# The second pass of the scores of windowed attention on all 128 rows of the array, in a two-layer hybrid block

## The chip, the cores and the metric

The kernel runs on one core of a Trainium2 chip. The metric is the device time of one execution in microseconds. The engines are named as the profile names them: PE is TensorE (PEld its loads of stationary operands), DVE is VectorE, ACT is ScalarE, POOL is GpSimd, and SP issues the DMAs.

## What is computed

The reference is a block of two layers over 256 context tokens and 512 latent tokens of 1024 channels. In each layer the modulated rows go through an input projection into four groups of heads: windowed attention with sinks, retention, RWKV-7 and latent attention. Their outputs are joined and projected, and an MLP follows. The part that the change is about is the windowed attention, four query heads on two key heads of 64 channels:

```python
def sink_softmax(s, sink):
    m = jnp.maximum(jnp.max(s, axis=-1, keepdims=True), sink)
    p = jnp.exp(s - m)
    return p / (jnp.sum(p, axis=-1, keepdims=True) + jnp.exp(sink - m))
...
    s_loc = jnp.einsum('bnqhgd,bnkhd->bhgnqk', qb, kb).astype(jnp.float32)
...
    s_loc = jnp.where(valid, s_loc, -jnp.inf)
    s_ctx = jnp.einsum('bnqhgd,bchd->bhgnqc', qb, kc).astype(jnp.float32)
    probs = sink_softmax(jnp.concatenate([s_loc, s_ctx], axis=-1),
                         sink_hg[None, :, :, None, None, None]).astype(v.dtype)
```

Each block of 128 latent queries sees the keys of its own block, of the blocks beside it within a window of 128, and all 256 keys of the context. In the first layer the context's queries attend to the context as well.

## The kernel before

**Stages.** For each layer, `run` calls `mixers` (the input projection, beside the RWKV recurrence), `attention`, `out` (the output projection) and `mlp`. `attention` first merges three streams of instructions: the end of the recurrence (`Rwkv.tail`), `mla_prep` and `swa_prep`, which load, rotate and split the queries and keys of the two attentions. Then it merges three more, each in proportion to its share of the work: `mla` (latent attention), `swa` (windowed attention), and a chain of `Rwkv.finish`, `ret` (retention) and `w_out`. A scheduler orders each engine's instructions after that, and gives each tile a buffer of its pool when it is first written.

**Two passes in float32r.** A float32 operand is split into a high part, as float32r, and a low part, which is the rest. `swa_prep` builds for each of two blocks of query heads a tile `sq` of 128 rows with two blocks of columns: in block j, the high part of head j of the block on that head's 64 rows, and the low part on the other 64 rows (L883 and L884). For the keys it builds `skh`, in which block j holds the high part of key head j on both halves of the rows (L878, four casts of 64x768 on ACT), and `skl`, which holds the low part of both key heads, each on its own 64 rows (L879, two subtractions on DVE).

**Scores.** `swa` works by units: a block of query heads g, a tile of 128 tokens t, and a parity j. `scores` takes two banks of PSUM. Its inner function `products` issues two products for a range of keys: the first pass multiplies `sq` block j on all 128 rows with `skh` block j, so that high and low parts of the queries meet the keys' high part; the second pass multiplies the 64 rows of the queries' high part with the keys' low part. In both the queries are the stationary operand. A unit of context tokens (t below 2) has one such pair, over 256 columns; a unit of latents has two, over the 256 context columns and over the two or three blocks of latent keys (256 or 384 columns), and then one or two mask products of 128 columns in bfloat16, which add the window's bounds. There are 24 units in the first layer and 16 in the second. `softmax` follows: the row's maximum on DVE (L657), the exponential on ACT (L663, tile `prob`), and the normalisation on DVE. `attend` issues the scores of a unit ahead of the transposes of the one before (tile `pt`), and after each second unit the products with the values.

**Buffers and loads.** Tiles of 128 rows by two blocks of 768 columns come from one pool of 17 buffers (tag D), tiles of 1024 columns from another of 16 (tag B). In the attention the D tiles are those of both preparations, of `Rwkv.finish` (`fin`), of retention (`ret`), the outputs `y`, and at the end the gates and rows of the output stage. Loads stand in one queue, SP's, in a fixed order; a load waits until the last user of its buffer is done, and the loads behind it wait too. Retention's loads for a pair of heads are its values (L948), its keys (L949), its decays (L951), its queries twice (L954) and its gate (L955).

All matrix products go through the helper `mm` (L148), all transposes through `tp` (L151).

Of the kernel before, what the change touches and what calls it, by code (L numbers as in the profile page):

```python
# [8 lines left out]
F32 = mybir.dt.float32  # L9
# [3 lines left out]
ALU = mybir.AluOpType  # L13
# [12 lines left out]
# blocks of 128 columns of the input projection, as kernel() lays them out  # L26
# [4 lines left out]
# per-channel parameters, one row per block of 128 channels  # L31
# [4 lines left out]
# channels of a windowed head: the first of each rotary pair, then the second  # L36
# [3 lines left out]
def const_arrays():  # L40
    """Arrays that depend on shapes alone."""
# [51 lines left out]
    # retention, per pair of heads: decays inside a chunk, then those of the queries (forward on top of backward)  # L93
# [15 lines left out]
def merge(*streams):  # L109
    """emit generators side by side, each in proportion to its share of its total"""  # L110
    live = [[g, 0.0, float(tot)] for g, tot in streams]
    while live:
        z = min(live, key=lambda z: z[1] / z[2])
        try:
            z[1] += next(z[0])
        except StopIteration:
            live.remove(z)


def in_proportion(*streams):  # L120
    """like merge, as a generator"""
    live = [[g, 0.0, float(tot)] for g, tot in streams]
    while live:
        z = min(live, key=lambda z: z[1] / z[2])
        try:
            c = next(z[0])
            z[1] += c
            yield c
        except StopIteration:
            live.remove(z)  # L130
# [7 lines left out]
class Block:  # L138
# [15 lines left out]
    def rebank(self, one, two):  # L154
        """the first `one` banks serve requests for one bank, the pairs at `two` those for two"""
# [10 lines left out]
    def ptok(self):  # L166
        """two banks as 768 token columns: the context ends the first bank, the latents fill the second"""
        return self.pb()[:, 256:1024]

    def done(self, ps):  # L170
        """the instructions so far are the last on what pr, pb or ptok gave"""
# [6 lines left out]
    def D(self, name, dt=F32):  # L178
        """two blocks of 768 columns"""
# [15 lines left out]
    def split(self, hi, lo, src, lo_eng=None, pin=False):  # L195
        """src = hi + lo exactly, hi with float32r's significand; pin: not ahead of what the engine was given
        before, since src is still being loaded"""
# [9 lines left out]
    def rsqrt_small(self, ss, n, eps):  # L207
        """(ss / n + eps) ** -0.5 for a [128, k] tile"""
# [7 lines left out]
    def head_sums(self, squares, tiles, mul, add, add_op):  # L216
        """squares: [128, T] blocks (two heads each); (mul * sum over the head + add) ** -0.5 per token, head
        and block, as [128, block, head, tile]"""
# [12 lines left out]
    def head_rstd(self, sq, tiles, mul, add, add_op):  # L231
        """(mul * sum of the squares over the head + add) ** -0.5 on every channel of the head, in PSUM"""
# [5 lines left out]
    def on_channels(self, col, n, tiles):  # L238
        """columns of values per token as rows, each repeated over 128 / n channels, in PSUM"""
# [24 lines left out]
    def start(self):  # L264
        """constants, silu of the conditions, the normalised rows; then the loads of the first modulation, whose
        blocks of channels the projection takes as they come"""
# [12 lines left out]
        # silu(c) and silu(c_ctx), channel-major, padded to 32 columns  # L279
# [12 lines left out]
        # adds up the four groups of 32 rows, and picks the two conditions  # L292
# [27 lines left out]
        def modulation(k):  # L320
            """A and B of a block of channels: the rows of the weights in four groups side by side, then their sum"""
# [36 lines left out]
    def params(self, l):  # L358
        """per-channel parameters of layer l, one column per block of 128 channels"""
# [22 lines left out]
        # sinks of the four heads, on every partition  # L382
# [7 lines left out]
    def ada(self, parts, n):  # L390
        """modulation columns into DRAM, n of them from each (layer, first column): weights times silu on the
        vector engine and the sum over the partitions on the tensor engine"""
# [41 lines left out]
    def modulation(self, l, gname, src):  # L434
        """A = gain * (1 + scale), B = shift, channel-major, for latent and context"""
# [22 lines left out]
    def x_norm(self, x, xhat, sq):  # L458
        """xhat = x / rms(x) for a token tile"""
# [6 lines left out]
    def make_hT(self, hT, xh, mod, tl, room, blocks=range(8)):  # L466
        """channel-major hi | lo of the modulated rows of the token tiles tl; room: 1024 spare columns"""
# [17 lines left out]
    def load_w(self, src, shape, pool=None):  # L485
        """hi, lo tiles of a weight block"""
# [20 lines left out]
    def proj(self, ps, wh, wl, hT, segs):  # L507
        """ps[c, tok] = sum over channel blocks of W^T h, three passes; yields its share of the time"""
# [12 lines left out]
    def split_pair(self):  # L521
        """the first pair of banks serves requests for one bank from now on"""
# [21 lines left out]
    def in_spilled(self, l, hT, emit):  # L544
# [14 lines left out]
        def load(i):  # L559
            """the weights of block i of the order"""  # L560
# [5 lines left out]
        def prepare(i):  # L566
# [3 lines left out]
            if b == "kpe":      # the two halves side by side  # L570
# [9 lines left out]
        def ahead(b, g):  # L580
            """the products of block b, with the split of the next weights in their midst"""
# [42 lines left out]
        # rotary part of the keys  # L624
# [28 lines left out]
    def softmax(self, ps, n, nsink, sink, scale):  # L653
        """ps [128 q, n] scores -> normalised probabilities in SBUF"""
# [18 lines left out]
    def transposed(self, p, n):  # L673
        """[128, n] -> [128 keys, n/128, 128 q] in SBUF"""
# [14 lines left out]
    def token_major(self, dst, x, how="ident"):  # L689
        """[128 c, T] -> [128 tokens, 6, 128 c], as it is or without each head's mean"""  # L690
# [14 lines left out]
    def attend(self, units, scores, values):  # L705
        """units (key, parity): the scores of a unit are under way while the one before is transposed"""
# [16 lines left out]
    def mla_prep(self, l, emit):  # L723
# [16 lines left out]
        # the gain of q goes into the rows of w_uq, 1/rms (per token) into the softmax's scale  # L740
# [24 lines left out]
        def rotate(x, r):  # L765
            """the latents of x[r], in place"""
# [42 lines left out]
        # values, token-major  # L809
# [38 lines left out]
    def swa_prep(self, l, emit):  # L848
# [6 lines left out]
        def load(x, xp, src, t0):  # L855
            """as it is, and with the rotary pairs' members swapped"""
# [12 lines left out]
        kh, kl = self.D("skh", F32R), self.B("skl", F32R)[:, 0:T]  # L869
        qs = []  # L870
        for x, xp, t0 in ((k, xs[0], 0), (qq[:, 0], xs[1], tq0), (qq[:, 1], xs[2], tq0)):
# [3 lines left out]
            if t0 == 0 and x is k:  # L875
                for j, r in enumerate(half):
                    for r2 in (r, half[1 - j]):
                        nc.scalar.copy(kh[r2, j], k[r])  # L878
                    nc.vector.tensor_tensor(kl[r], k[r], kh[r, j].bitcast(F32), ALU.subtract)  # L879
            else:       # hi of a head where it is, lo on the other half of the partitions  # L880
# [9 lines left out]
    def swa(self, l, emit):  # L890
# [4 lines left out]
        def scores(key, j):  # L895
# [3 lines left out]
            r = slice(64 * j, 64 * j + 64)  # L899
# [3 lines left out]
            def products(out, keys, stop):  # L903
                self.mm(out, q, kh[:, j, keys], True, False)
                self.mm(out, q[r], kl[r, keys], False, stop)
# [27 lines left out]
    def ret(self, l, emit):  # L933
        """chunks of 128 tokens, both directions at once; the mean over a head's channels is taken from the
        values, which the outputs are linear in"""
# [886 lines left out]
```

## Time and profile before

| | |
|---|---|
| median of 3 runs | 2292.72 us (2283.75 to 2300.33) |
| span of the profiled execution, first to last instruction | 2293.7 us |
| PE busy | 2178.0 us, 95% of the span |
| DVE, ACT, POOL busy | 61%, 32%, 28% |
| attention, layer 0 and layer 1 | about 480 to 710 us and 1700 to 1885 us |

The profile tells the profiled execution's time as its span alone, which lies within the range of the three runs, 1.0 us above their median. Busy time counts an instruction from its start to its end. Products overlap in the array, so the time that one takes from the next is the step between their starts, which the timeline shows, and not its own duration. The granted clock of PE is given as a share: 1.0 is 2.4 GHz, 0.5 is 1.2 GHz.

### The profile page before, as it was taken

What the parts mean: (1) busy time and instruction counts of PE and PEld (TensorE: products, weight loads), DVE (VectorE), ACT (ScalarE), POOL (GpSimd) and SP (SyncE); (2) the same over time, 40 slices, a digit from 0 to 9 for tenths busy, and PEclk for the clock granted to TensorE, in tenths of its full rate; (3) what the DMA queues carried; (4) which work ended last, traced back from release to release, by engine and by line L of the source; (5) the groups of instructions that cost most, each with busy time, mean ns of one, the idle gap of its engine ahead of it and who ended that gap; (6) DMA issues with size and microseconds to landing.
All of it is one profiled execution on the core that took longest, in us unless ns stands there. A gap on an engine that the chain in (4) does not pass through costs nothing. (4 is left out here: it accounts for less than half of the span.)

```text
span 2293.7 us, 36538 instructions
## 1 busy us (share of the span) xinstructions
PE 2178.0 (95%) x14420; PEld 1671.5 (73%) x14420; DVE 1396.8 (61%) x2708; ACT 739.1 (32%) x1356; POOL 635.7 (28%) x711
## 2 busy tenths in 40 slices
PE   7998999989999999999999899999998999999997
PEld 4865666656667988888888686566666667888886
DVE  5488788767574766556555655777776555333334
ACT  3232222244443422222222333222233344332331
POOL 2443323240122311212112354322341013221321
PEclk9999999988899999999999999899999799999999
DMA  6322233431124444444343321111232123332232
GB/s 263 100 92 89 90 113 95 132 111 42 47 82 149 142 130 141 133 147 143 122 129 113 133 85 70 46 54 53 76 109 71 38 88 137 111 120 83 96 107 101
DMA packets 110889, 239.91 MB, mean 105 GB/s; under 512 B 22834, under 2 KB 49276, under 8 KB 110716
## 3 DMA queue, kind: packets, MB, share of 16 engines
q1 hardware_dynamic: 110716, 237.57, 31.6%
q8 instruction: 113, 1.85, 0.3%
q14 instruction: 60, 0.49, 0.1%
HBM read 206.93 MB, written 30.58 MB: 104 GB/s over the span
## 5 line engine op out<-in xcount | busy, mean ns | idle before, releaser
L148 PE MATMUL ps<-y,whi 128*128 128x512 f32 (+1 forms) x1664 | 422.1, 343 | 2.3 <-POOL y L482 1.0
L148 PE MATMUL ps<-whi,f 128*128 128x512 f32 x1280 | 401.0, 392 | 3.3 <-DVE f L1191 3.3
L148 PE MATMUL ps<-hT,whi 128*128 128x512 f32 (+3 forms) x1360 | 392.5, 370 | 5.2 <-ACT st L606 2.0
L198 ACT CAST whi<-wraw 128x1024 fp32r<-128x1024 f32 (+1 forms) x176 | 182.5, 1041 | 610.1 <-PE ps L148 377.7
L148 PEld LDWEIGHTS ps<-y,whi 128*128 128x128 f32 x1664 | 290.1, 190 | 42.6 <-POOL y L482 2.6
L148 PEld LDWEIGHTS ps<-hT,whi 128*128 128x128 f32 (+1 forms) x1360 | 232.9, 191 | 78.6 <-issue 37.8
L148 PE MATMUL ps<-y,wlo 128*128 128x512 f32 (+1 forms) x832 | 283.4, 342 | 0.7 <-POOL wlo L201 0.6
L148 PEld LDWEIGHTS ps<-whi,f 128*128 128x128 f32 x1280 | 240.9, 188 | 57.6 <-DVE f L1191 4.1
L201 POOL TENSOR_TENSOR wlo<-wraw,whi 128x1024 fp32r<-128x1024 f32 x57 | 141.1, 2475 | 428.8 <-ACT whi L198 403.2
L201 DVE TENSOR_TENSOR wlo<-wraw,whi 128x1024 fp32r<-128x1024 f32 x117 | 152.2, 1303 | 165.0 <-ACT whi L198 164.6
L148 PE MATMUL ps<-wlo,f 128*128 128x512 f32 x640 | 249.8, 390 | 0.0
L148 PE MATMUL ps<-hT,wlo 128*128 128x512 f32 (+1 forms) x648 | 233.7, 361 | 0.8 <-DVE wlo L201 0.8
L415 DVE SCALAR_TENSOR_TENSOR aacc<-aw,sil,aacc 128x768 f32<-128x768 f32 x140 | 162.2, 1204 | 27.6 <-ACT aacc L413 19.8
L148 PEld LDWEIGHTS ps<-y,wlo 128*128 128x128 f32 x832 | 157.8, 190 | 19.1 <-POOL wlo L201 0.8
L1190 POOL TENSOR_TENSOR fr<-fr 128x768 f32<-128x768 f32 (+1 forms) x64 | 92.9, 1451 | 272.0 <-ACT f L1189 265.4
L148 PEld LDWEIGHTS ps<-hT,wlo 128*128 128x128 f32 x648 | 125.3, 193 | 27.5 <-issue 11.7
L1191 DVE TENSOR_TENSOR f<-fr,f 128x768 fp32r<-128x768 f32 (+1 forms) x64 | 63.5, 992 | 123.7 <-POOL fr L1190 123.7
L148 PEld LDWEIGHTS ps<-wlo,f 128*128 128x128 f32 x640 | 120.6, 188 | 24.5
L1217 DVE TENSOR_TENSOR ya<-ya,ps 128x1024 f32<-128x1024 f32 x60 | 72.9, 1217 | 96.2 <-PE ps L148 96.2
L148 PE MATMUL ps<-wo,y 128*128 128x512 f32 x480 | 117.1, 397 | 3.8 <-POOL wo L201 1.9
L1604 DVE STREAM_TRANSPOSE Xp<-XY 32x128 f32<-32x128 f32 x384 | 115.8, 302 | 5.3
L148 PEld LDWEIGHTS ps<-wo,y 128*128 128x128 f32 x480 | 88.1, 188 | 25.3 <-ACT wo L198 4.0
(308 smaller groups left out, 3364.5 us busy)
## 6 DMA issues: line engine op xcount, KB each, us to landing
wraw<-in_w_b_dram SPq DMA_DIRECT2D x64, 512.0 KB
wraw<-in_mlp_w_dram SPq DMA_DIRECT2D x64, 512.0 KB
aw<-in_ada_w_dram SPq DMA_DIRECT2D x80, 384.0 KB
wraw<-in_w_in_b_dram SPq DMA_DIRECT2D x46, 512.0 KB
ada<-in_ada_w_dram SPq DMA_DIRECT2D x64, 192.0 KB
adaw<-in_ada_s_dram SPq DMA_DIRECT2D x16, 512.0 KB
wraw<-in_w_out_k_dram SPq DMA_DIRECT2D x32, 256.0 KB
xs<-x SPq DMA_DIRECT2D x16, 512.0 KB
```

The costliest lines, as they stand in the source:

```text
L148: self.nc.tensor.matmul(ps, lhsT, rhs, start=start, stop=stop)
L198: ins = self.nc.scalar.copy(hi, src)
L201: (lo_eng or self.nc.vector).tensor_tensor(lo, src, hi.bitcast(F32), ALU.subtract)
L415: nc.vector.scalar_tensor_tensor(a, w, sil, a, ALU.mult, ALU.add)
L1190: nc.gpsimd.tensor_tensor(fr, fr, fr, ALU.mult)
L1191: nc.vector.tensor_tensor(fl, fr, fh.bitcast(F32), ALU.subtract)
L1217: nc.vector.tensor_tensor(ya[t], ya[t], ps, ALU.add)
L1604: nc.vector.transpose(Xp[r, zz, b], Y[r, zz])
```

## The change

The keys' low part gets the layout of their high part: `skl` becomes a tile of the D pool with two blocks of columns, and block j holds the low part of key head j on both halves of the rows. DVE writes it on the head's own rows, as before, and ACT copies it to the other 64 rows. The second pass then multiplies all 128 rows of `sq` block j, the same stationary operand as the first pass has, with block j of `skl`. With it the product of both low parts, which was left out before, is added to the scores.

```diff
@@ swa_prep
-        kh, kl = self.D("skh", F32R), self.B("skl", F32R)[:, 0:T]
+        kh, kl = [self.D(nm, F32R) for nm in ("skh", "skl")]
@@
                 for j, r in enumerate(half):
                     for r2 in (r, half[1 - j]):
                         nc.scalar.copy(kh[r2, j], k[r])
-                    nc.vector.tensor_tensor(kl[r], k[r], kh[r, j].bitcast(F32), ALU.subtract)
+                    nc.vector.tensor_tensor(kl[r, j], k[r], kh[r, j].bitcast(F32), ALU.subtract)
+                    nc.scalar.copy(kl[half[1 - j], j], kl[r, j].bitcast(F32))
@@ swa, scores
-            r = slice(64 * j, 64 * j + 64)
             ps = self.ptok()
             q = qs[g][:, j, 128 * t:128 * t + 128]
...
             def products(out, keys, stop):
                 self.mm(out, q, kh[:, j, keys], True, False)
-                self.mm(out, q[r], kl[r, keys], False, stop)
+                self.mm(out, q, kl[:, j, keys], False, stop)
```

One line is added, so lines from L880 to the end of the scores stand one lower in the changed kernel until the removed line evens it out: the casts of the queries are L883 before and L884 after.

How instructions move: on PE, DVE and ACT the order changes only within the preparation of each layer; after it each engine has the same order as before. On ACT, in the preparation of the first layer, the rows before, from the casts of the keys on (`mla` belongs to latent attention, `ot` and P, T to the recurrence, `mqk` are the latent attention's queries):

```order
L878 CAST skh<-swa 64x768 x4
L762 COPY mla<-ps 128x768
L1695 COPY ot<-ps 128x256
L883 CAST sq<-swa 64x768 x2
L793 ACTIVATE mqk<-ps 64x768
L1671 COPY P_556<-ps 64x256
L793 ACTIVATE mqk<-ps 64x768
L1676 COPY T_558<-ps 64x256
L883 CAST sq<-swa 64x768 x2
L1695 COPY ot<-ps 128x256
```

and the same place in the changed kernel:

```order
L878 CAST skh<-swa 64x768 x4
L880 CAST skl<-skl 64x768
L762 COPY mla<-ps 128x768
L880 CAST skl<-skl 64x768
L1695 COPY ot<-ps 128x256
L884 CAST sq<-swa 64x768 x2
L793 ACTIVATE mqk<-ps 64x768 x2
L1671 COPY P_556<-ps 64x256
L884 CAST sq<-swa 64x768 x2
L1676 COPY T_558<-ps 64x256
```

The two added casts stand behind those of the keys, ahead of the first copy of `ot`, and the first two copies of `mqk` now stand together.

On SP, the loads of the recurrence's outputs and of the first pair of retention heads in the first layer, with what each waits for, before (DMAHW names other DMAs; a buffer's number stands in the tile's name):

```order
L1752 DMA fin_4895<-sp_rwv0_159 128x768 [waits DMAHW7_49,PE_49]
L1753 DMA fin_4895<-sp_rws0_160 128x768 [waits DMAHW0_49]
L948 DMA ret_5063<-sp_ret0_157 128x768 [waits DMAHW2_49,DMAHW1_49,DVE_49]
L949 DMA ret_5061<-sp_ret0_157 128x768 [waits PE_49]
L951 DMA ret_5061<-sp_ret0_157 128x768 [waits DMAHW3_49]
```

and in the changed kernel:

```order
L1752 DMA fin_4897<-sp_rwv0_159 128x768 [waits DMAHW4_49,DVE_49]
L1753 DMA fin_4897<-sp_rws0_160 128x768 [waits DMAHW0_49]
L948 DMA ret_5065<-sp_ret0_157 128x768 [waits DMAHW1_49,PE_49]
L949 DMA ret_5063<-sp_ret0_157 128x768 [waits DMAHW2_49,DMAHW0_49,DVE_49]
L951 DMA ret_5063<-sp_ret0_157 128x768 [waits DMAHW3_49]
```

The order is the same; the wait for PE has moved from the keys' load (L949) to the values' load in front of it (L948). The buffer that is waited for is the one that held `Rwkv.finish`'s gates, whose last reader is a product on PE. The second layer has the same exchange.

## Rows read from the trace of the kernel before

**Rows 1.** The page: busy time, share of the span, instructions.

```profile
PE 2178.0 (95%) x14420; PEld 1671.5 (73%) x14420; DVE 1396.8 (61%) x2708; ACT 739.1 (32%) x1356; POOL 635.7 (28%) x711
```

**Rows 2.** Stretches: length, busy PE, PEld, DVE, ACT, POOL, granted clock, DMA.

```profile
480.00:710.00 230.00, 210.67 (x1374) 150.33 (x1375) 146.05 (x370) 100.10 (x246) 44.32 (x30) 0.90 0.23 74
1700.00:1885.00 185.00, 165.96 (x1142) 119.09 (x1143) 114.75 (x285) 78.05 (x178) 34.81 (x23) 0.90 0.19 60
...
591.60:608.70 17.10, 16.79 (x73) 12.07 (x72) 7.78 (x24) 5.30 (x17) 4.03 (x2) 0.50 0.00 1
584.00:591.60 7.60, 5.75 (x43) 3.44 (x39) 3.30 (x11) 3.19 (x11) 0.00 (x0) 1.00 0.55 154
```

**Rows 3.** Tiles skl and skh: duration ns min/median/max, starts, forms.

```profile
L148 PEld LDWEIGHTS ps<-skl,sq x72: 182/183/286, 488.0 to 1855.8; 64*128 64x128 f32 x72
L148 PE MATMUL ps<-skl,sq x72: 278/382/686, 488.0 to 1855.8; 64*128 64x256 f32 x56, 64*128 64x384 f32 x16
...
L878 ACT CAST skh<-swa x8: 818/830/832, 472.5 to 1700.9; 64x768 fp32r<-64x768 f32 x8
```

**Rows 4.** Timeline of PE, one unit of latents: start us, us, instruction.

```profile
559.10 0.38 PE L148 MATMUL ps<-skh,sq 128*128 128x256 f32 x1 [0.82 <-ACT prob L663]
559.41 0.38 PE L148 MATMUL ps<-skl,sq 64*128 64x256 f32 x1
559.72 0.44 PE L148 MATMUL ps<-skh,sq 128*128 128x384 f32 x1
560.09 0.44 PE L148 MATMUL ps<-skl,sq 64*128 64x384 f32 x1
560.47 0.29 PE L148 MATMUL ps<-msk 128*128 128x128 bf16 x2
```

**Rows 5.** Timeline of the weight loads, the same unit.

```profile
559.41 0.18 PEld L148 LDWEIGHTS ps<-skl,sq 64*128 64x128 f32 x1
```

**Rows 6.** Timeline of PE, input projection, one block of weights.

```profile
93.01 0.39 PE L148 MATMUL ps<-hT,wlo 128*128 128x512 f32 x1
93.24 0.40 PE L148 MATMUL ps<-hT,whi 128*128 128x256 f32 x2
93.47 0.28 PE L148 MATMUL ps<-hT,wlo 128*128 128x256 f32 x1
...
95.99 0.28 PE L148 MATMUL ps<-hT,wlo 128*128 128x256 f32 x1
```

**Rows 7.** Timeline of the weight loads, the same block.

```profile
93.36 0.19 PEld L148 LDWEIGHTS ps<-hT,wlo 128*128 128x128 f32 x1
```

**Rows 8.** Timeline of PE, part of a unit at clock 0.50.

```profile
607.62 0.58 PE L148 MATMUL ps<-skh,sq 128*128 128x256 f32 x1
608.13 0.58 PE L148 MATMUL ps<-skl,sq 64*128 64x256 f32 x1
```

**Rows 9.** Waits of PE, 495:710 then 1720:1885: us, times, longest.

```profile
PE ps L148 <- ACT prob L663: 5.7, 7, 1.8
PE ps L148 <- POOL hr L228: 3.0, 3, 1.9
...
PE ps L148 <- ACT prob L663: 3.1, 2, 2.4
```

**Rows 10.** Timeline of ACT, preparation of layer 0, then of layer 1.

```profile
476.49 0.36 ACT L1695 COPY ot<-ps 128x256 f32<-128x256 f32 x1
478.81 1.68 ACT L883 CAST sq<-swa 64x768 fp32r<-64x768 f32 x2 [1.96 <-DVE swa L874]
...
1703.97 0.80 ACT L762 COPY mla<-ps 128x768 f32<-128x768 f32 x1 [2.22 <-PE ps L148]
```

**Rows 11.** Timeline of SP, layer 0: retention's values and keys.

```profile
526.75 0.32 SPq L948 DMA_DIRECT2D ret<-sp_ret  x1
547.84 0.32 SPq L949 DMA_DIRECT2D ret<-sp_ret  x1
```

**Rows 12.** Timelines of PE and POOL, layer 0: first uses of those loads.

```profile
552.16 1.50 PE L148 MATMUL ps<-cst,ret 128*128 128x128 f32 x12
...
556.04 1.81 POOL L969 TENSOR_TENSOR ret<-ret,retc 128x768 f32<-128x768 f32 x1 [14.07 <-DMA ret<-sp_ret]
```

## The prediction

> **What bounds the kernel now.** I read the page first: TensorE (PE) is busy 95% of the span [rows 1]. Then the busy time by stretch, for the two stretches in which the windowed attention runs, one per layer [rows 2]: there PE is busy 210.67 of 230 us and 165.96 of 185 us, VectorE 63% and 62%, ScalarE less. So PE sets the pace in these stretches and waits only 38 us in both together. The list of PE's waits says for what: mostly for ScalarE's exponentials, which free the banks that the next scores go to, and for a small POOL result [rows 9]; none lasts over 2.4 us. What PE saves there should mostly arrive at the end, less what turns into such waits.
>
> The view of one tile counts the changed products: 72 second-pass products on 64 rows, 56 of 256 columns and 16 of 384 [rows 3]. The timeline of PE then shows what they cost: not their columns, but the step from one shape of the array to another. From the start of a first-pass product (128 rows) to the second-pass product (64 rows) it is 0.31 us for 256 columns and 0.37 us for 384, and from there back to 128 rows again 0.31 and 0.38 us [rows 4]. The weight load of the second pass starts with its product, at 559.41, and not ahead of it [rows 5]: the load of 183 ns [rows 3] lies open at each change of shape. In the input projection, where every product is 128 rows by 128 columns and has its own load, products of 256 columns start every 0.12 us ((95.99 - 93.24) / 23 steps), and of 512 columns 0.23 us apart [rows 6]; the load for the product at 93.47 starts at 93.36, under the one before [rows 7]. There the same weights stand twice running (the rows with x2), and each product loads them anew; over the whole kernel, too, there are as many loads as products [rows 1]. So equal weights spare no load, they only leave the shape as it is.
>
> **The change part by part.**
>
> PE. Nothing is removed or added; the 72 products get 128 rows, so each stays in the shape of its neighbours. A unit of latents (16 in each layer, 32) goes through four such steps, 559.10 to 560.47 = 1.37 us; at the steps of [rows 6] it would be 0.12 + 0.12 + 0.175 + 0.175 = 0.59 us (384 columns taken midway between 0.12 and 0.23). So a step saves 0.19 us. I count the steps in the program's order, which after the preparation is the same before and after. Into the second pass: 63 come from the first pass (12.0 us), 6 from transposes of 128 columns, which are of full shape too and save about half, 0.09 each (0.5 us), and 3 from other places (nothing taken). Out of it: 25 go to the next first pass, 22 to the mask, 11 to transposes, 2 to other full products, 60 x 0.19 = 11.4 us; the other 12 go mostly to products of 64 columns or 96 rows, where the shape changes anyway (nothing taken). Together 23.9 us at the full clock, 2.4 GHz. Some 18 of these steps, counted by the clock at their start, fell in stretches at 1.2 GHz, where one takes 0.51 us [rows 8] against an estimate of 0.24 (twice 0.12): 0.08 us more each, 1.4 us. Sum 25.3 us of PE time.
>
> A mask product behind a 128-row product doesn't stand in the trace of before; its step lies between 0 (the load wholly hidden) and today's 0.31 to 0.38. I take it as any full product's; were all 22 as they are, 4.2 us would go.
>
> How much arrives: each wait of PE that remains can swallow what was won since the scores that it depends on were issued, about one unit's 0.78 us at most. The two lists name 21 and 15 waits, 12 of them in the three groups of [rows 9]. At 36 x 0.78 us all would be lost, at none nothing; since the chain behind a wait begins with scores that come earlier too, I take 30% as lost. That leaves 17.7 us, with 25.3 and 10 as ends.
>
> ScalarE. Four casts of 64x768 are added, two per layer, at 0.83 us as their likes take [rows 3]. In layer 0 they stand behind the four casts of the keys: there ScalarE ends at 476.85 and is idle 1.96 us until 478.81, waiting for VectorE [rows 10], so 1.66 us fit; in layer 1 there is an idle of 2.22 us [rows 10]. They cost nothing if they come that early. If that cover is gone, they push what is queued behind them (the copy of the recurrence's outputs, the casts of the queries, the copies of the latent attention's queries) by 1.66 us a layer, and PE waits for these copies: 3.3 us. VectorE does the same work in another order: between a gain and a loss of 1 us. I take 0.5 us in all.
>
> Buffers and SP. The low part now holds one of the 17 buffers of two blocks for the whole attention, so later tiles get other ones. SP's order of loads is the same but for one pair, but a wait moves: the values of the first pair of retention heads, until now issued at 526.75 when a VectorE result freed their buffer, now wait for PE, as the keys did, which were issued at 547.84 [rows 11]. Behind them on SP stand the keys and the rest of retention's loads, which lose only the time of one issue, 0.32 us. First used are the values at 552.16, by PE [rows 12]: 4.3 us after the new issue. All these loads together had landed by 556.04, when POOL's wait for the last one needed ended [rows 12], so the values take between nothing and 8.2 us: PE stands still between 0 and 3.9 us, in each layer. As they are first in the queue, I take 0.5 us each, 1.0 in all.
>
> Sum: 17.7 - 0.5 - 1.0 = 16.2 us off the profiled 2293.7 us, and with a little for the clock (below) 17.7: 2276 us. The profiled span lies 1.0 us above the median of the three runs, 2292.72, so both give the same ratio, 0.7% less. About 1% (23 us) is what a measurement of this kernel can tell from no change, as its three runs spread over 16 us.
>
> **The rivals.**
>
> All arrives, and the clock rises with it. From 591.6 to 608.7 us the granted clock is 0.50, the 1.2 GHz level, and PE is busy 16.79 us of it; in the 7.6 us ahead of the fall it was busy 5.75 us [rows 2]. After the change the same columns go through in less time, without open loads between, and one or two such falls may not come: each saves half of its busy time, some 8 us. Then 2293.7 - 25.3 + 1.5 - 8 = 2262 us. For it: PE bounds these stretches. Against it: softmax is in series with it, and a PE that waits more can lose clock as well. This is why I add 1.5 us only to the sum.
>
> The loads stay open, and the change does not do what it says. Then PE saves nothing, and casts and loads cost 1.5 us: 2295 us. Against it speak [rows 6, 7], which show loads hidden between products on the same 128 rows, also with equal weights; only these very tiles were never seen in that order.
> The Trainium skill, "TensorE: Matmul & The Clock Gate", section "Part 3: Packing small matmuls — row/col tiling", has a rule by which this would be so: weight loads overlap with products under way only where their row groups differ, and 128 rows after 128 rows share all of theirs. The trace here disagrees, with a load that starts 0.11 us ahead of its product.
>
> The chain of softmax takes the place of the loads. VectorE is busy only 63%, but its steps stand one behind another between scores and transposes. If PE's waits swallow three quarters, 6.3 us arrive: 2293.7 - 6.3 + 1.5 = 2289 us. For it: the waits for exponentials are there already [rows 9].
>
> Slower: the values of retention come late. If they take the whole 8.2 us, PE, which is in order, stands 3.9 us still, and if it then falls to the half clock for 17 us as in [rows 2], that costs some 8.5 us more: 12.4 us a layer, 24.8 in all, and 2293.7 - 17.7 + 0.5 + 24.8 = 2301 us. It outweighs the gain from 8.6 us per layer on. Against it: PE's transposes of the values are the first use of five loads, and the others were not waited for by PE.
>
> **How the numbers follow.** Chances: the forecast 0.55, all with the clock 0.24, softmax 0.10, loads stay open 0.06, late values 0.05. The forecast's own range is 2268 to 2284 us, by 10 to 25.3 us gained. The whole range, 2258 to 2291 us, takes in the first three cases and leaves out the open loads, the late values and the far end of the clock, some 0.15 to 0.2. Faster by over 1% means below 2270 us: most of the second case and a little of the first, 0.28. Slower by over 1% is the far end of late values, 0.05. The rest, 0.67, is within 1%.
>
> **What would show it.** In the profile after: second-pass products on 128 rows, their loads starting ahead of them; steps from first to second pass near 0.12 us and a latents' unit near 0.6 us; fewer open steps but more or longer waits of PE for exponentials in the two stretches, which should be 9 to 10 us shorter in layer 0 and 7 to 8 in layer 1. The casts should start within 2 us of the keys' casts, and no PE wait should name the values' load. The prediction is wrong if the steps stay at 0.31 us, if the stretches shrink by under 5 us together though the steps fall, or if half-clock time there changes by more than 17 us.

## The result, and the profile after

The changed kernel takes 2270.68 us (median of 4 runs, 2269.23 to 2272.71) against 2296.26 us of the kernel before beside it (4 runs, 2283.75 to 2300.33): a ratio of 0.9898, 95% interval 0.987 to 0.9927. A later set of runs gave 2269.48 against 2293.41 us, 0.9885 (0.9848 to 0.9922). The forecast was 2276 us, 16.7 us or 0.7% less; measured are 24 to 26 us, 1.0 to 1.15%. The 2276 lies 5 us above the measured time, inside the range. What made it come out so is another sum than the one that was written.

The page, line of busy time, as in [rows 1]; the span is 2267.4 us, 26.3 less than before:

```profile
PE 2144.2 (95%) x14420; PEld 1654.3 (73%) x14420; DVE 1404.1 (62%) x2708; ACT 741.5 (33%) x1360; POOL 639.7 (28%) x711
```

PE has the same 14420 products and is busy 33.8 us less. Where, the two stretches of attention tell. From here on a stretch runs from the last product of a layer's input projection to the first of its output projection, so that it holds the same work in every kernel. Columns as in [rows 2]: length, then PE, PEld, DVE, ACT, POOL busy, granted clock, DMA. First before, then after:

```profile
457.20:672.60 215.40, 197.38 (x1333) 138.63 (x1332) 143.99 (x359) 92.79 (x230) 47.76 (x28) 0.87 0.22 69
1689.10:1865.00 175.90, 157.90 (x1102) 112.65 (x1101) 113.27 (x279) 72.85 (x166) 37.47 (x23) 0.88 0.20 63
```

```profile
458.70:661.50 202.80, 179.54 (x1332) 132.33 (x1331) 148.08 (x359) 94.27 (x232) 48.18 (x28) 0.90 0.23 73
1679.00:1840.80 161.80, 140.10 (x1101) 103.15 (x1100) 113.26 (x279) 74.50 (x168) 37.64 (x23) 0.94 0.22 68
```

The stretches are 12.6 and 14.1 us shorter, which is the whole difference; PE is busy 35.6 us less in them (355.3 to 319.6) and idle 8.9 us more. And the granted clock rose, from 0.87 and 0.88 to 0.90 and 0.94. Added up from the trace's record of the granted clock, PE stood at 1.2 GHz for 95.6 us of the two stretches before and for 61.5 us after. That is one execution of each, but the others agree. The share of the clock that wasn't granted, times the span (the clock's loss from here on; half of the time at 1.2 GHz), is 78.5 us in the mean of 17 executions of the kernel before and 60.5 us in the mean of six of the change beside them, in the later set of runs, where the mean times differ by 25.9 us.

The changed products, as in [rows 3] (min/median/max ns, starts, forms):

```profile
L148 PEld LDWEIGHTS ps<-skl,sq x72: 186/189/336, 490.1 to 1831.7; 128*128 128x128 f32 x72
L148 PE MATMUL ps<-skl,sq x72: 276/282/684, 490.3 to 1831.8; 128*128 128x256 f32 x56, 128*128 128x384 f32 x16
...
L880 ACT CAST skl<-skl x4: 825/830/831, 475.8 to 1692.1; 64x768 fp32r<-64x768 f32 x4
```

The load takes 189 ns, against 183 on 64 rows; what fell is the product's median, 382 to 282 ns, as most loads now start ahead of their product. One unit of latents on PE, as in [rows 4], and its loads, as in [rows 5]:

```profile
555.65 0.36 PE L148 MATMUL ps<-skh,sq 128*128 128x256 f32 x1
555.85 0.28 PE L148 MATMUL ps<-skl,sq 128*128 128x256 f32 x1
555.97 0.34 PE L148 MATMUL ps<-skh,sq 128*128 128x384 f32 x1
556.14 0.34 PE L148 MATMUL ps<-skl,sq 128*128 128x384 f32 x1
556.33 0.28 PE L148 MATMUL ps<-msk 128*128 128x128 bf16 x2
```

```profile
555.62 0.19 PEld L148 LDWEIGHTS ps<-skh,sq 128*128 128x128 f32 x1
555.73 0.19 PEld L148 LDWEIGHTS ps<-skl,sq 128*128 128x128 f32 x1
...
556.32 0.11 PEld L148 LDWEIGHTS <-msk 128*128 128x128 bf16 x2 [0.16 <-issue]
```

The unit takes 0.68 us (555.65 to 556.33) instead of 1.37. Three steps are 0.12, 0.17 and 0.19; the first is 0.20. The second pass's load starts at 555.73, 0.12 us ahead of its product; the first pass's starts at 555.62, only 0.03 ahead, behind transposes that follow each other every 0.11 us and so are shorter than a load. The mask's load, in bfloat16 behind products in float32, starts with its product as before (556.32 and 556.33), although the rows are the same: not only a change of row count leaves a load open. No run tells what does it there.

PE's waits in the same two stretches (us in all, times, longest; layer 0, then layer 1), as in [rows 9]:

```profile
PE ps L148 <- ACT prob L663: 8.0, 8, 2.2
PE ps L148 <- POOL hr L228: 3.6, 3, 1.7
PE ps L148 <- ACT T L1676: 2.9, 1, 2.9
...
PE ps L148 <- ACT prob L663: 4.5, 3, 2.4
PE ps L148 <- POOL hr L228: 3.4, 4, 1.3
```

The waits for exponentials grew from 5.7 to 8.0 and from 3.1 to 4.5 us, 3.7 of the 8.9 us that PE is idle longer, and no wait of PE over 0.15 us in these stretches names a DMA. ScalarE's preparation in layer 0, as in [rows 10], and the loads of retention on SP with PE's first use of them, as in [rows 11, 12]:

```profile
473.24 2.53 ACT L878 CAST skh<-swa 64x768 fp32r<-64x768 f32 x3
475.78 0.83 ACT L880 CAST skl<-skl 64x768 fp32r<-64x768 f32 x1
...
477.44 0.83 ACT L880 CAST skl<-skl 64x768 fp32r<-64x768 f32 x1
```

```profile
522.29 0.32 SPq L1752 DMA_DIRECT2D fin<-sp_rwv  x1
...
545.43 0.32 SPq L948 DMA_DIRECT2D ret<-sp_ret  x1
546.06 0.32 SPq L949 DMA_DIRECT2D ret<-sp_ret  x1
```

```profile
549.75 1.50 PE L148 MATMUL ps<-cst,ret 128*128 128x128 f32 x12
```

The casts stand where the forecast put them, within 2 us of the keys' casts. The values' load moved from 526.75 to 545.43, as forecast, and nobody on PE waited for it. One more wait moved that the prediction doesn't name: the load at L1752, part of the recurrence's outputs, went out at 522.29; before it went out at 501.24.

### The profile page after: what moved, and what is told of

It reads as the page before. It is cut to its first block, busy times and chain, and to the rows that moved or that the text cites. A ratio compares the mean times of both kernels' runs of the same rounds, so it can differ in the third digit from the quotient of the medians.

```text
span 2267.4 us, 36543 instructions
## 1 busy us (share of the span) xinstructions
PE 2144.2 (95%) x14420; PEld 1654.3 (73%) x14420; DVE 1404.1 (62%) x2708; ACT 741.5 (33%) x1360; POOL 639.7 (28%) x711
## 5 line engine op out<-in xcount | busy, mean ns | idle before, releaser
L148 PEld LDWEIGHTS ps<-hT,wlo 128*128 128x128 f32 x648 | 125.0, 193 | 27.4 <-issue 11.7
```

The lines of the kernel that those rows point to most:

```text
L148: self.nc.tensor.matmul(ps, lhsT, rhs, start=start, stop=stop)
```

## The experiments

Twelve runs were made, of ten further kernels: e12 is e4's kernel once more, e13 the change itself. Half clock is the time at 1.2 GHz. It and the two columns behind it are of one profiled execution each, and the two are worked out by one rule: a step is the time from one product's start to the next one's; what the trace records as idle in it is put under idle, and the rest of the steps that begin at a score or mask product under scores. All are sums over the two stretches, in us. Each ratio is to runs of the kernel before made beside the run, whose medians lie between 2292.6 and 2296.3 us.

| kernel | median us (range, runs) | ratio to before, 95% | half clock, layers 0 / 1 | scores | PE idle |
|---|---|---|---|---|---|
| before | 2296.26 (2283.75–2300.33, 4) | – | 54.6 / 41.0 | 56.0 | 36.0 |
| the change | 2270.68 (2269.23–2272.71, 4) | 0.987–0.9927 | 41.0 / 20.5 | 34.7 | 45.0 |
| e1_half_rows | 2295.94 (2292.35–2299.40, 10) | 0.9996–1.0031 | 58.0 / 47.8 | 55.5 | 34.6 |
| e2_other_weights | 2267.03 (2265.41–2271.64, 4) | 0.9857–0.9928 | 37.5 / 20.5 | 34.7 | 44.4 |
| e3_zero_low | 2269.74 (2266.20–2278.17, 5) | 0.987–0.9934 | 37.5 / 20.5 | 34.6 | 42.4 |
| e4_two_b_tiles | 2261.59 (2259.02–2263.65, 4) | 0.9828–0.9909 | 30.7 / 20.5 | 33.7 | 42.4 |
| e5_layer0_only | 2284.14 (2280.21–2285.52, 6) | 0.9949–0.9975 | 44.4 / 41.0 | 43.6 | 40.8 |
| e7_both_on_64 | 2289.49 (2278.55–2295.79, 10) | 0.9961–1.0 | 61.4 / 44.4 | 37.7 | 39.9 |
| e8_two_b_zero | 2270.40 (2268.39–2272.74, 4) | 0.989–0.9921 | 37.5 / 34.1 | 34.6 | 41.5 |
| e9_two_b_64 | 2295.48 (2284.50–2306.03, 10) | 0.9993–1.0034 | 41.0 / 44.4 | 54.6 | 36.1 |
| e10_split_64 | 2301.06 (2295.24–2309.43, 12) | 1.0006–1.005 | 85.3 / 44.4 | 69.0 | 28.6 |
| e11_split_128 | 2274.46 (2272.12–2280.57, 6) | 0.9878–0.9946 | 47.8 / 20.5 | 44.7 | 38.9 |
| e12_two_b_again | 2265.22 (2262.33–2267.15, 6) | 0.9832–0.9899 | 34.1 / 27.3 | 33.8 | 42.8 |
| e13_change_again | 2269.48 (2265.71–2271.57, 6) | 0.9848–0.9922 | 41.0 / 20.5 | 34.7 | 43.7 |

### Is it the rows? Half rows in the change

```diff
+            r = slice(64 * j, 64 * j + 64)
...
-                self.mm(out, q, kl[:, j, keys], False, stop)
+                self.mm(out, q[r], kl[r, j, keys], False, stop)
```

Here and below `r` is the 64 rows of head j; a second pass on them leaves the low part of the queries times the low part of the keys out, as before the change.

> The changed kernel in all but one thing: the second pass multiplies only the head's own 64 rows of sq and of the new skl, so the array changes shape as before; layout, casts, buffers and the order on PE are those of the change. Theory (the gain is the shape of the array): PE's steps at the scores return to 0.31 and 0.37 us, and the time to that of the kernel before plus what preparation and buffers cost, within 5 us of it, ratio 0.998 to 1.003, with about as much half-clock time in the two attention stretches as before (54.6 and 41.0 us; after the change 41.0 and 20.5). Rival (new buffers and the new order made the gain): the time stays near the changed kernel's 2270 us. Rival (the half-clock time of the one execution profiled before was chance): the half-clock time stays near 61 us in both stretches together, and the time is about 2282 us.

With casts, buffers and PE's order as in the change, but 64 rows in the second pass, the time is before's again: 2295.94 us, 25.3 above the change. The two stretches:

```profile
458.10:674.00 215.90, 198.54 (x1334) 140.43 (x1332) 142.40 (x359) 94.67 (x232) 48.46 (x28) 0.87 0.21 69
1687.70:1866.20 178.50, 161.25 (x1102) 114.30 (x1100) 114.92 (x279) 74.65 (x168) 37.62 (x23) 0.87 0.19 62
```

The unit that took 0.68 us takes 1.34 again, and the clock is back at 0.87 as well. So the shape of these 72 products carries the whole gain, the clock's part included; order, buffers and casts carry none of it.

### Do equal weights matter?

```diff
+            q2 = qs[g][:, 1 - j, 128 * t:128 * t + 128]
...
-                self.mm(out, q, kl[:, j, keys], False, stop)
+                self.mm(out, q2, kl[:, j, keys], False, stop)
```

> The changed kernel, but the second pass takes the other block of sq as its stationary operand (the scores are then sums of two different heads' products, so the result is not the reference's): 128 rows as in the change, but not the first pass's weights. Theory (shape alone): the time of the changed kernel within 4 us, steps of 0.12 us at full clock between second pass and next first pass. Rival (equal weights spare a load or part of it): the steps grow by up to 0.19 us at each of 72 places, and the time goes up by 8 to 14 us.

The second pass gets the other head's queries as weights, so the scores mix two heads. 2267.03 us, and score steps of 34.7 us as in the change: the first pass's weights are not what helps, the first pass's shape is.

### Do the casts cost anything?

```diff
+        for j, r in enumerate(half):
+            nc.gpsimd.memset(kl[half[1 - j], j].bitcast(F32), 0.0)
...
-                    nc.scalar.copy(kl[half[1 - j], j], kl[r, j].bitcast(F32))
```

> The changed kernel without the four casts on ACT: the other 64 rows of each block of skl are zeroed by POOL ahead of time, so the product of the low parts is left out, as before the change. Theory (the casts lie in idle time of ACT): the time of the changed kernel within 3 us. Rival (the casts delay the preparation): 3 to 5 us less, with the first transposes of probabilities 1 to 3 us earlier in each layer.

The other 64 rows are zero, and the low part of the queries times the low part of the keys is left out. 2269.74 us, the change's time: the four casts cost nothing that can be seen. Without them VectorE and ScalarE have the order of the kernel before, and PE has it but for about ten rows, so this run also shows the gain without the change's new order.

### Does the clock follow the shape, layer by layer?

```diff
+                if l == 0:
                     self.mm(out, q, kl[:, j, keys], False, stop)
+                else:
+                    self.mm(out, q[64 * j:64 * j + 64], kl[64 * j:64 * j + 64, j, keys], False, stop)
```

> The second pass on 128 rows in layer 0 alone; in layer 1 on 64 rows, with everything else as in the change. If the gain comes from the steps between shapes, and the clock follows them stretch by stretch, layer 0's stretch (from the last product of the input projection to the first of the output projection) is as in the change, about 203 us, and layer 1's as with 64 rows, about 178 us instead of 162; the total is some 14 to 17 us above the change, 2283 to 2287 us. If the clock follows chance or what happened in the layer before, layer 1's half-clock time needn't go back up to some 45 us, and the total lies elsewhere between 2270 and 2296 us.

```profile
456.00:659.20 203.20, 181.58 (x1334) 134.78 (x1332) 145.45 (x359) 94.17 (x232) 47.77 (x28) 0.89 0.23 73
1677.20:1854.30 177.10, 157.92 (x1102) 111.83 (x1100) 115.35 (x279) 74.63 (x168) 38.08 (x23) 0.88 0.19 62
```

203.2 and 177.1 us: layer 0 as in the change, layer 1 as with half rows, in length and in clock (0.88). The median, 2284.14, lies where the first theory put it. The clock gained in a stretch goes with that stretch's own products.

### A change of shape, or 64 rows as such?

```diff
-                self.mm(out, q, kh[:, j, keys], True, False)
-                self.mm(out, q, kl[:, j, keys], False, stop)
+                self.mm(out, q[r], kh[r, j, keys], True, False)
+                self.mm(out, q[r], kl[r, j, keys], False, stop)
```

> Both passes on 64 rows: the first pass takes one head's 64 rows of the queries' high part too, so the low part of the queries times the high part of the keys is left out. If a change of shape is what leaves a load open, a second pass right behind its first one comes about 0.12 us after it for 256 columns and 0.18 for 384, while the steps out of a pair to the mask, transposes and other products of 128 rows stay at some 0.3, and so do the steps into it; the total lies between the change and before, about 2280 to 2290 us, as half of the steps are still open. If any product on 64 rows waits for its own load, the steps stay at 0.22 to 0.31 inside the pair too and the total is that of before, 2293 us or more.

Now no shape changes inside a pair of passes, at half the rows. One unit of latents:

```profile
560.15 0.38 PE L148 MATMUL ps<-skh,sq 64*128 64x256 f32 x1
560.37 0.28 PE L148 MATMUL ps<-skl,sq 64*128 64x256 f32 x1
560.49 0.33 PE L148 MATMUL ps<-skh,sq 64*128 64x384 f32 x1
560.66 0.33 PE L148 MATMUL ps<-skl,sq 64*128 64x384 f32 x1
560.93 0.28 PE L148 MATMUL ps<-msk 128*128 128x128 bf16 x2
```

The steps are 0.22, 0.12, 0.17 like the change's; only the step out of the pair, to 128 rows, is 0.27 instead of 0.19. So products on 64 rows hide their loads among themselves, and between these products in float32 it is the change of shape that opens one. Scores take 37.7 us against 55.5 with half rows, 17.8 less. The changes of shape on the way into a pair, which the table has not under scores, take 6.4 us of it back: 54 steps from other products, 14.6 against 8.2 us. PE's idle time takes another 5.3 (34.6 to 39.9). That leaves 6.1, and 6.4 us arrive (2295.94 to 2289.49): the clock gives nothing, with 105.8 us at 1.2 GHz in the one and in the other. The change, whose pairs have neither step open, is another 19 us below, with 61.5 us at 1.2 GHz. The profiled execution of this kernel is among the slowest of its ten, but over all ten the clock's loss is 79.4 us in the mean, against 78.2 over the ten with half rows: no clock came back in the others either.

### Open loads with nearly full rows

```diff
-                self.mm(out, q, kl[:, j, keys], False, stop)
+                r, o, k0 = slice(64 * j, 64 * j + 64), out, keys.start
+                self.mm(o[:, 0:16], q[r], kl[r, j, k0:k0 + 16], False, False)
+                self.mm(o[:, 16:], q, kl[:, j, k0 + 16:keys.stop], False, stop)
```

e11_split_128 differs from this in one line: its product of 16 columns is on 128 rows, with `q` and `kl[:, j, ...]`.

> As the change, but the second pass is taken in two products: the first 16 columns on one head's 64 rows (there the low part times the low part is left out), the rest on 128 rows. So nearly all columns have full rows, and the changes of shape are back: two per pair of passes. Against the next run, which has the same order and 128 rows throughout. If the granted clock follows the open loads, half-clock time in the two stretches goes up to about 106 us as with half rows, and the total lies some 40 us above the next run; if it follows the rows that are multiplied, half-clock time stays near 62 us, and the total lies only the open loads above it, 72 x 2 x 0.11 to 0.19 = 16 to 27 us, less what waits take.

> The same 72 further products of 16 columns, on 128 rows: no change of shape, the arithmetic of the change. 72 products at some 0.03 us each make 2 us: 2271 to 2277 us, with half-clock time near the change's 62 us. If further products that are short break the overlap of loads even in one shape, 72 x 0.07 to 0.19 us are added, 2276 to 2284 us.

The two have the same order on every engine. Stretches of e10_split_64, then of e11_split_128:

```profile
459.00:685.10 226.10, 210.38 (x1374) 154.97 (x1372) 146.68 (x360) 94.71 (x232) 48.70 (x28) 0.81 0.21 66
1701.60:1877.00 175.40, 162.51 (x1132) 118.26 (x1131) 117.48 (x280) 74.48 (x168) 38.29 (x23) 0.87 0.20 63
```

```profile
457.10:661.80 204.70, 184.27 (x1374) 140.39 (x1372) 142.73 (x360) 94.26 (x232) 48.94 (x28) 0.88 0.23 73
1678.30:1841.30 163.00, 144.49 (x1134) 107.08 (x1132) 116.89 (x280) 74.62 (x168) 37.92 (x23) 0.94 0.21 68
```

72 more products on 128 rows cost 4 to 5 us (2274.46). With them on 64 rows the time is 26.6 us higher. The score steps differ by 69.0 - 44.7 = 24.3 us, 0.17 us for each of 144 changes of shape; the steps that begin at neither a score nor a mask product take 19 us longer, at a clock of 0.81 and 0.87; and PE's idle time gives 10 us of it back. (The profiled execution of e10_split_64 is 6 us above its median.) The total came out where "the clock follows the rows" had put it, and the clock did the opposite: half-clock time is 129.7 us, not near 62, though 240 of 256 columns have full rows. Over all executions the clock's loss is 85.3 us in the mean of twelve, against 66.7 in six of e11_split_128.

Taken with the run before: the half clock returns in every kernel that has products on 64 rows among the scores, with about half of the open loads (e7) or with nearly all columns on full rows (e10). In layer 1 it is 41.0 to 47.8 us in the six kernels with 64-row products there and 20.5 to 34.1 us in the eight without. In layer 0 the groups touch: 41.0 to 85.3 against 30.7 to 47.8. What in these products the clock answers to, the runs don't tell.

### The low part in two small tiles

```diff
-        kh, kl = [self.D(nm, F32R) for nm in ("skh", "skl")]
+        kh, kl = self.D("skh", F32R), [self.B("skl", F32R)[:, 0:T] for _ in range(2)]
...
-                self.mm(out, q, kl[:, j, keys], False, stop)
+                self.mm(out, q, kl[j][:, keys], False, stop)
```

> The changed kernel, with the two blocks of skl in two tiles of the other pool, so that the D tiles and retention's loads get the buffers and waits of the kernel before (values ahead of the keys). Theory (the moved wait costs nothing): the time of the changed kernel within 3 us. Rival (the values' load came late and cost up to 3.9 us a layer): 2 to 8 us less than the changed kernel.

The low part no longer takes one of the 17 large buffers, and the loads on SP go out as before the change:

```profile
496.17 0.32 SPq L1752 DMA_DIRECT2D fin<-sp_rwv  x1
...
516.51 0.32 SPq L948 DMA_DIRECT2D ret<-sp_ret  x1
535.07 0.32 SPq L949 DMA_DIRECT2D ret<-sp_ret  x1
```

2261.59 us, 9 us below the change and so more than either of the two expectations, most of it in layer 0 (194.5 against 202.8 us). Four more runs were to tell what that is.

> The kernel with two small tiles for the low part once more, beside the change on the same chip. If its 9 us are its own: 2259 to 2264 us, 0.4% below the next run. If they came from the chip or the job of that run, it is within 2 us of the next run.

> The change itself once more, as the measure for the three runs before: 2269 to 2273 us.

Side by side the small tiles take 2265.22 and the change 2269.48 us. The means of six runs differ by 4.5 us, with an interval of about 2.7 either way worked out from the spread of the runs: a gain, and a smaller one than first seen.

```profile
457.50:656.20 198.70, 176.47 (x1332) 130.48 (x1332) 144.38 (x359) 94.06 (x232) 46.83 (x28) 0.91 0.23 75
1670.50:1834.50 164.00, 143.41 (x1101) 105.91 (x1100) 113.89 (x279) 74.16 (x168) 38.10 (x23) 0.92 0.21 67
```

In layer 0 it is 3 us ahead of e13 (198.7 against 201.9) and in layer 1 2.4 behind. Over the six executions of each the clock's loss is 55.1 against 60.5 us, as much as the gain.

The same small tiles with 64 rows in the second pass (same order on every engine as e4):

```diff
-                self.mm(out, q, kl[j][:, keys], False, stop)
+                self.mm(out, q[64 * j:64 * j + 64], kl[j][64 * j:64 * j + 64, keys], False, stop)
```

> The low part in two tiles of one block as in the kernel with two small tiles (2261.6 us), so that loads and buffers stand as before the change, but the second pass on 64 rows. If the shape's gain and the cost of the large buffer add, this lies as far above that kernel as the half-rows run lay above the change, 25 us: 2286 to 2290 us, some 6 to 9 us below the half-rows run and below before (the two tiles and two casts more leave it a little off before's). If the 9 us that two small tiles won come only together with the full rows (by the clock), it lies at 2293 us or above.

2295.48 us, no less than the half-rows kernel with the large buffer (2295.94). Without the full rows the small tiles bring nothing, so the loads that go out earlier are not worth 9 us by themselves. And with zeros in place of the casts (the diff is against the change):

```diff
+        for j, r in enumerate(half):
+            nc.gpsimd.memset(kl[j][half[1 - j]].bitcast(F32), 0.0)
...
-                    nc.vector.tensor_tensor(kl[r, j], k[r], kh[r, j].bitcast(F32), ALU.subtract)
-                    nc.scalar.copy(kl[half[1 - j], j], kl[r, j].bitcast(F32))
+                    nc.vector.tensor_tensor(kl[j][r], k[r], kh[r, j].bitcast(F32), ALU.subtract)
```

> Two small tiles, and the other head's 64 rows set to zero by POOL in place of the four casts, so the low part of the queries times the low part of the keys is left out, as before the change. If the casts cost nothing, as the run with zeros on the large buffer says, the total is that of the kernel with two small tiles, 2259 to 2264 us; if the casts delay the end of the preparation in layer 0, it is 2 to 4 us less, about 2258 us. If POOL's zeros, which come before the keys are there, delay POOL's part of the preparation, it is above 2264 us.

2270.40 us: the gain of the small tiles is gone, with PE idle no longer than in e4 (41.5 against 42.4 us) but 71.6 us at the half clock against 51.2. The expectation laid a time above 2264 us to POOL; longer idle of PE, which that would need, isn't there. Over 100 rows of PE's order differ from e4's, so the two differ in more than the casts. The better likeness is e3, the zeros on the large buffer: it has the same order on VectorE and ScalarE and all but some 16 rows of it on PE. There the values' load went out at 545.80, here at 526.62, and the times are the same, 2269.74 and 2270.40 us: in this order the large buffer costs nothing. What the 4 to 9 us of the small tiles hang on stays open; they show as clock, in one order and not in another. The kernel with the two small tiles is the fastest that ran: 0.9869 and 0.9865 of before.

## Why the prediction was right, and where not

**The steps of PE** were the right mechanism. The forecast took 25.3 us; the score steps fell by 56.0 - 34.7 = 21.3. Three terms were off. The step from the first to the second pass was taken to fall from 0.31 to 0.12 us for 256 columns; its median over 44 such steps at the full clock is 0.22. It is 0.12 in the median of the nine where the first pass follows another second pass, and the steps of 384 columns, nearly all of that kind, came out as taken (0.18). Behind other work, most often transposes, it is 0.20 to 0.22 and more: there, as in the unit above, the first pass's own load starts just ahead of its product and seems to lie partly open, whatever comes after it. So the projection of [rows 6], where each product is long enough to hide the next load, was the wrong likeness. The steps out of the second pass to the first came out as taken (0.31 to 0.12). Those to the mask, taken as any full product's, measure 0.17 in the median against 0.31, with the mask's load still open. And the steps to latent-attention products of 96 rows, for which nothing was taken since "the shape changes anyway", fell from 0.31 to 0.12 as well, in medians over a few starts (three before, four after): 96 rows did not open a load beside 128. Some 3 us of the 21.3 are clock, as 5.9 us less of the score steps ran at 1.2 GHz.

**The rule on loads.** The rival of the open loads is refuted by the very tiles: a load at 555.73, its product at 555.85, and no less than 0.11 us between them in any of the 57 pairs at the full clock. By the rule of the Trainium skill, "TensorE: Matmul & The Clock Gate", section "Part 3: Packing small matmuls — row/col tiling", that load shares all its row groups with the product under way and should have waited; the runs disagree, on 128 rows and on 64 (e7). Another page of the Trainium skill fits: "TensorEngine Tiling (Array Packing)", "Key Properties", says that a change of tiling mode drains the engine. It gives no price; e10 against e11 gives 0.17 us for each change. No trace shows a drain as such, only the load that starts late.

**The waits** were forecast to swallow 30%, 7.6 us. PE's idle time rose by 8.9 us. The prediction read [rows 9] as mostly exponentials, but these were 8.8 of 36.0 us; they are the largest single wait, and took 3.7 us of the rise, a wait for the recurrence's T in layer 0 another 2.6 (0.3 to 2.9). The steps less the waits then give 21.3 - 8.9 = 12.4 us, not 17.7.

**ScalarE's casts and the values' load** were priced at 1.5 us. The casts cost nothing (e3), no wait of PE names the load, and the late-values rival didn't happen. Whether the large buffer costs anything isn't settled: small tiles won 4 to 9 us in e4's order and nothing in e8's, where the load went out 19 us earlier as well.

**The clock** is the term that failed. The prediction added "1.5 us only to the sum", since "a PE that waits more can lose clock as well". PE did wait more, and half-clock time fell by 34.1 us all the same, twice the 17 us that the prediction had named as the mark for being wrong. The steps that begin at neither a score nor a mask product, and so belong to work that wasn't changed, took 14.2 us less (299.2 to 285.0). Most of it is clock: 27.4 us less of them ran at 1.2 GHz, and half of that is 13.7. So the books read 21.3 - 8.9 + 14.2 = 26.6 us in the stretches, against 17.7 forecast: 5.3 too much for steps and waits, 12.7 too little for the clock, 1.5 too much for costs. That the total still fell into the range is luck in part, since errors of both signs met; by the prediction's own mark its account of the clock was wrong. The stretches shrank by 12.6 and 14.1 us, not by 9 to 10 and 7 to 8. The rival in which the clock rises took 8 us for it and would have been nearer there, but had the waits at nothing.

That the fall isn't chance, e1, e5 and e13 show: with 64 rows the clock is lost again, in one layer alone if only that layer has them, and kept where the change is run again. The loss over all executions says the same (78.5 and 60.5 us), and by it up to 18 of the 25.9 us are clock. That not every shortened step brings clock with it, e7 shows: about half of the open loads gone gave 6.4 us and no clock.

## What to carry to other kernels

Where products of different row counts alternate on TensorE, count the changes of shape: each left a load open, 0.17 us in the mean of 144, and filling an operand's unused 64 rows with something useful or with zeros removed it at no price in columns. Take the steps after the edit from the same neighbours, since a load behind short transposes or before a bfloat16 mask stayed open here all the same. Look up the granted clock of the stretch before and after such an edit and give it a term of its own size, since here it gave back at least as much again as the steps less the waits. Test the buffers that an edit takes apart from the edit, and with more than one order of instructions: two small tiles in place of one large one were worth a few us more in one order and nothing in another.

## What the runs showed that was not expected

Products on 64 rows among products on 128 go with a lower granted clock, and not in proportion to the loads that they leave open: e7 has as much half-clock time as the half-rows kernel, 105.8 us, with 11 us less of such steps. Some kernels with 64-row products scatter widely, and with the clock: before ran from 2283.58 us at a mean clock of 0.970 to 2312.31 us at 0.959 over 17 executions, e9 by 21.5 us over ten and e7 by 17; the change by 3.5 and 5.9 over four and six. It is no rule, as e1 varies by 7 over ten and e3, on 128 rows, by 12 over five. A load hides on 64 rows as well as on 128 as long as the shape stays, and 96 rows behaved as 128 do in the few steps there are.
